# A two-layer recurrent and attention trunk on one core: split weights in their own tiles, other banks, norm sums on VectorE, masks at once, sixteen unread matmuls

## The chip, the core and the metric

The kernel runs on one core of a Trainium2 chip. The core has a matrix engine (TensorE, "PE"; its weight loads are listed as "PEld"), VectorE ("DVE"), ScalarE ("ACT"), GpSimd ("POOL") and SyncE ("SP"), whose queue issues nearly all transfers here. The metric is the device time of one launch in microseconds (us). The kernel before took 2058.51 us, the median of 3 runs from 2057.19 to 2059.92.

## The reference

Input and output are 512 tokens of 2048 features in float32. There are two residual layers.

- Layer A (HGRN2): RMS norm; one product with a 2048 x 8192 weight gives q, the forget logits, v and a gate; a gated linear recurrence in 16 heads of 128; a norm per head; times SiLU of the gate; a 2048 x 2048 output product; plus the residual.
- Layer B (forgetting attention): RMS norm of the new stream; keys, values and forget sums from one weight, queries and a gate from another; causal softmax attention in 16 heads with a decay term; a norm per head; times SiLU of the gate; a 2048 x 2048 output product; plus the residual.

```
proj = rmsnorm(x, norm_w) @ w_in
o = head_rmsnorm(recurrence_or_attention(...), out_norm_w)
x = x + (o * silu(gate)) @ w_out
```

All products are needed to float32 accuracy. The kernel splits each operand into a high part (rounded to the matrix engine's type) and a low part (the rest) and adds three products: high by high, high by low and low by high.

## The kernel before, in words

Activations are kept as 16 tiles of 128 features x 512 tokens. A *group* (function `group`, line 215) computes 512 output columns: 16 steps of 128 input features, each with 12 matmuls of 512 columns into four PSUM banks (three matmuls for each bank). At step 0 the group takes the banks gm0 to gm3; after step 15 `evac` empties each bank. There are 16 groups in stage "a" (the projections of layer A), 16 in stage "b", and an output product behind each.

*Weights.* `Chunks.load` (184) brings 512 KB, two steps' worth, into one of two raw buffers `wr` through SP's queue. `w_split` (139) makes the parts: ACT casts `wh`, DVE subtracts to get `wl` (`split`, 434: ACT in line 435, DVE in line 436; in stage b with scales, lines 147 and 148). Its tiles come from `w_tiles` (134): three of each in the pool of the current stage, two in the output products, where the same tag also serves the larger parts of the seven-product groups. `phase` (77) closes the pool of a stage and opens the next one on the same memory; a tile of the new pool waits for those tiles of the old one that lie where it lies.

*Output products* (`out_product`, 826). The first 512 outputs are a plain group; beside it `y_split` (780) splits the gated head outputs `Y`, and `quick_prep` (249) forms, for each pair of steps, sums of the quarters of two tiles in `tm` (one buffer), three subtractions on DVE and one on POOL, and splits them to `th` and `tl`. The other 1536 outputs are six *seven-product groups* (`quick_groups`, 311, and `quick`, 264), each with 8 steps of 21 matmuls of 256 columns; this is Strassen's scheme in Winograd's form on 2 x 2 blocks. `w_sums` (153) forms the sums of the weight quarters in `wm`, `w_split_quick` (160) splits them. `quick_sum` (295) puts the seven products together: one copy on ACT (299) and seven operations on DVE (300 to 309), with three temporaries `t`. Groups 0, 2 and 4 use the gm banks, groups 1, 3 and 5 the four `mx` banks (`bank`, 70). The last evacuation of layer A's product is held back and called in the third step of stage b's first group (`last_a`, line 849).

*Norms* (`Norm`, 337). `add` squares a tile on ACT (349) and adds it to a running sum on POOL (350); `finish` sums over partitions on PE. The first norm is added up in `load_x` (464) in the first group of stage a, beside the split of x (469, 470). The second is added up in `x1_done` (805), as each tile of the new stream X1 comes out of layer A's product. `x1_split` (847) splits X1 in the first group of stage b and calls `finish` in the last step.

*The start.* SP is asked for two tiles of x (256 KB each), the first weights (512 KB), two more tiles of x, and eight small vectors. Ten masks for the recurrence are made by POOL (a fill and two selections each, 514, 515 and 519) and cast by DVE (523), one mask for each step of the first group from the fourth on (`setup`, 472).

*Order.* Besides the groups, generators (`mix_a`, 599, and `mix_b`, 914) hold the work of the heads; `pump` advances them by so many pieces for each step. The program is laid down in this order, and a planner (`schedule_with_timeline_sim`, line 1087) then sets each engine's order for good: an instruction that is early in the program comes first, and a later one is moved into a gap where the plan has its operands and its tile ready. On the chip each engine follows its order and waits where the plan was too early. `hold` (226) keeps the last step of a stage from splitting the first weights of the next.

Of the kernel before, what the change touches and what calls it, by code (L numbers as in the profile page):

```python
# [10 lines left out]
F32R = mybir.dt.float32r  # L11
U8 = mybir.dt.uint8
# [4 lines left out]
P = 128  # L17
T = 512
D = 2048
KT = 16  # L20
H = 16
# [11 lines left out]
def hgrn2_fox(ctx, tc, io):  # L33
    nc = tc.nc
# [5 lines left out]
    cur = {}  # L40
# [4 lines left out]
    def nt(tag, shape, bufs, dt=F32, pool=None):  # L45
        uid[0] += 1
        return padded(pool or sb, shape, dt, tag, f"{tag}_{uid[0]}", bufs)
# [10 lines left out]
    def const(tag, shape, dt=F32):  # L58
        return padded(cp, shape, dt, tag, tag)
# [5 lines left out]
        return t.bitcast(F32)  # L65

    def tmp():
        return mt("t", (P, T), 4)

    def bank():  # L70
        return nt("mx", (P, T), 4, pool=ps)

    def mt(tag, shape, bufs=1, dt=F32):

        return nt(tag, shape, bufs, dt, cur["sb"])

    def phase(name):
        if cur:
            cur["ctx"].close()
        cur["ctx"] = c = ExitStack()  # L80
        cur["quick"] = name[0] == "o"
        cur["sb"] = c.enter_context(tc.tile_pool(name=f"sb{name}", bufs=1, reuse_waits="tile"))

    phase("a")
# [46 lines left out]
    load_vec("a_norm_w", S)  # L131


    def w_tiles(shape):

        n = 2 if cur["quick"] else 3
        return mt("wh", shape, n, F32R), mt("wl", shape, n, F32R)

    def w_split(r, kt, scales):
        h, l = w_tiles((P, T))  # L140
        if scales is None:
            split(r, h, l)
        else:
            n = T // len(scales)
            for i, w in enumerate(scales):
                c = slice(i * n, (i + 1) * n)
                S.activation(h[:, c], r[:, c], AF.Copy, scale=w[:, kt : kt + 1])  # L147
                V.scalar_tensor_tensor(  # L148
                    l[:, c], r[:, c], w[:, kt : kt + 1], rd(h)[:, c], op0=ALU.mult, op1=ALU.subtract
                )  # L150
        return h, l
# [8 lines left out]

    def w_split_quick(r, m):

        h, l = w_tiles((P, 2, 7, P))
        split(r[:, :, 1:4, :], h[:, :, 0:3, :], l[:, :, 0:3, :])
        split(m, h[:, :, 3:7, :], l[:, :, 3:7, :])
        return [(h[:, i, :, :], l[:, i, :, :]) for i in range(2)]

    class Chunks:
# [12 lines left out]
            for k in range(KT // 4):  # L181
                self.todo.append((ap[k], True, None, 0))

        def load(self):

            if not self.todo:
                return
            ap, quick, scales, kt = self.todo.pop(0)
            r = nt("wr", (P, 2 * T), 2)
            nc.sync.dma_start(r, ap)  # L190
            if quick:
                self.raw.append((lambda r=r.rearrange("p (a b c) -> p a b c", a=2, c=P): w_split_quick(r, w_sums(r)), 2))
            else:
                for i in range(2):
                    self.raw.append((lambda v=r[:, i * T : (i + 1) * T], k=kt + i: [w_split(v, k, scales)], 1))

        def split(self):
            if self.raw:
                fn, _ = self.raw.pop(0)
                self.parts.extend(fn())  # L200
# [48 lines left out]
    def quick_prep(p, y):  # L249

        k1, k2 = 2 * p, 2 * p + 1
        b11, b12, b21, b22 = y[k1][:, :TN], y[k1][:, TN:], y[k2][:, :TN], y[k2][:, TN:]
        m = mt("tm", (P, 4, TN), 1)
        V.tensor_sub(m[:, 0, :], b12, b11)
        G.tensor_sub(m[:, 2, :], b12, b22)
        V.tensor_sub(m[:, 1, :], b22, m[:, 0, :])
        V.tensor_sub(m[:, 3, :], b21, m[:, 1, :])
        th = mt(f"th{p}", (P, 3, TN), 1, F32R)
        tl = mt(f"tl{p}", (P, 3, TN), 1, F32R)
        split(m[:, 0, :], Xh[k1][:, TN:], Xl[k1][:, TN:])  # L260
        split(m[:, 1:4, :], th, tl)
        return th, tl
# [48 lines left out]
    def quick_groups(prep, residual, evac, hold):  # L311

        for u in range(6):
            k = 4 + 2 * u
            r = [residual(k), residual(k + 1)]
            banks = [nt(f"gm{j}", (P, T), 1, pool=ps) if u % 2 == 0 else bank() for j in range(4)]
            end = quick(banks, prep, lambda *p, k=k, r=r: evac(k, r, p), hold and u == 5)
            if u < 5:
                end()
        return end  # L320
# [16 lines left out]
    class Norm:  # L337
# [6 lines left out]
        def add(self, x):  # L344
            if self.n == 0:
                S.activation(self.acc, x, AF.Square)
            else:
                q = nt("z", (P, T), 4)
                S.activation(q, x, AF.Square)
                G.tensor_add(self.acc, self.acc, q)  # L350
            self.n += 1

        def finish(self):
# [98 lines left out]
    def fetch_x():  # L452
        kt = len(xs)
        if kt < KT:
            xs.append(nt(f"y{kt}", (P, T), 1))
            nc.sync.dma_start(xs[kt], io["x"][kt])

    for kt in range(2):
        fetch_x()
    wts.load()  # L460
    fetch_x()
    fetch_x()

    def load_x(kt):
        fetch_x()
# [37 lines left out]
    setup.append(lower_bounds)  # L503


    def mask(name, m, d, q0):
        n = 4 - q0
        g = P // (4 * m)
        u = const(name, (P, g * n * m), U8)

        def make():
            f = tmp()
            fv = f[:, : g * n * m].rearrange("p (g q r) -> p g q r", g=g, q=n)
            G.memset(f[:, : g * n * m], 1.0)
            G.affine_select(
                out=fv, in_=fv, pattern=[[-4 * m, g], [-m, n], [0, m]], compare_op=ALU.is_ge,
                fill=0.0, base=m * (d - q0), channel_multiplier=1,
            )
            G.affine_select(
                out=fv, in_=fv, pattern=[[4 * m, g], [m, n], [0, m]], compare_op=ALU.is_ge,  # L520
                fill=0.0, base=m * (q0 - d) + m - 1, channel_multiplier=-1,
            )
            V.tensor_copy(u, f[:, : g * n * m])

        setup.append(make)
        return u

    masks = {(1, 0): mask("m1_0", 1, 0, 0)}
    for m in (1, 4, 16):
        for d in (1, 2, 3):  # L530
            masks[m, d] = mask(f"m{m}_{d}", m, d, d)
    ats = [const(f"at{i}", (P, NW, P)) for i in range(2)]
    setup.append(lambda: [V.memset(t, 0.0) for t in ats])

# [269 lines left out]

    def x1_done(kt):
        nc.sync.dma_start(x1_d[kt], X1[kt])
        norm1.add(X1[kt])

    def out_a_evac():
        res = [res_a(j) for j in range(4)]  # L810
# [36 lines left out]
    def x1_split(kt):  # L847
        if kt == 2:
            last_a()
        if kt == 6:  # L850
            forget_weights()
        h, l = new_x(kt)
        split(X1[kt], h, l)
        X1[kt] = None
        if kt == KT - 1:
            norm1.finish()
# [2 lines left out]
    wfs = mt("wfs", (P, KT, 48), 1, F32R)  # L859

    def forget_weights():
        wf = mt("t", (P, KT, H), 4)
        nc.sync.dma_start(wf, io["wb_f"])
        V.memset(wfs.bitcast(F32), 0.0)
        V.tensor_mul(wf, wf, view(nk, 0, [[1, KT], [0, H]]))
        V.tensor_copy(wfs[:, :, 0:H], wf)
        V.tensor_sub(wfs[:, :, 32 : 32 + H], wf, rd(wfs)[:, :, 0:H])
# [224 lines left out]
```

## Time and profile before

The profiled execution took 2057.41 us, of which its span is 2055.4.

| quantity | value |
|---|---|
| PE busy | 1986.9 us, 97% |
| DVE busy | 1585.9 us, 77% |
| ACT busy | 1133.1 us, 55% |
| POOL busy | 305.6 us, 15% |
| mean granted clock of PE | 0.987 |
| bytes moved | 195 MB, 95 GB/s |
| PE idle for weight parts cast by ACT (`wh`) | 36.5 us in 3 waits |

How to read it. A row of the order of time is: start in us, duration in us, engine, line of the kernel, operation, output<-inputs, shapes and, behind "x", how many instructions are merged. In brackets stands the idle time of the engine ahead of it and what ended that. Matmuls overlap, so a matmul's duration (0.39 us) is longer than its distance to the next (0.23). The waits list the idle time of one engine by what ended it: total, times, longest. The stages list busy time of each engine between two times, with the granted clock of PE (1.00 is full, about half is the lowest seen) and what the transfers did. A row of one line gives the minimum, median and maximum duration in ns, the first and last start in us, and the shapes.

### The profile page before, as it was taken

Reading aid. Unit: us, or ns where it says so; the run is one execution under the profiler, and the core shown is the slowest. Engines: PE = TensorE matmul, PEld = TensorE weight load, DVE = VectorE, ACT = ScalarE, POOL = GpSimd, SP = SyncE. Lnnn points to the kernel's source line nnn. Section 1 sums busy time; section 2 is a strip of 40 time slices with the busy share of each in tenths; the row PEclk is TensorE's granted clock in tenths of the full one; section 3 lists DMA queues with packets and bytes.
Section 4 is the critical chain, followed back from the end, with each engine's and each line's share of the span. In section 5 each row is a group of like instructions: output and inputs, shape, how many; then the busy total and the mean of one; then the engine's idle time right before and its main releaser. Section 6 shows DMA issues by size and latency. Waiting matters only on the chain.

```text
span 2055.4 us, 28924 instructions
## 1 busy us (share of the span) xinstructions
PE 1986.9 (97%) x10202; PEld 1696.2 (83%) x10202; DVE 1585.9 (77%) x3250; ACT 1133.1 (55%) x2312; POOL 305.6 (15%) x404
## 2 busy tenths in 40 slices
PE   7999999999999999889999999999999999997998
PEld 5888888888888888779987888888888888885898
DVE  8778977989799889688984667666766666687787
ACT  5656655656566466644453555554555556564333
POOL 7303210313133031121110000010001000011000
PEclk9999999999999999989999999999999999998999
DMA  5222222222222222234433233223222322222453
GB/s 170 88 83 74 71 84 81 75 80 83 74 81 72 73 83 73 81 96 151 159 115 95 91 93 97 88 79 101 93 88 92 92 90 90 90 86 72 135 173 103
DMA packets 61408, 195.01 MB, mean 95 GB/s; under 512 B 7872, under 2 KB 8000, under 8 KB 61264
## 3 DMA queue, kind: packets, MB, share of 16 engines
q1 hardware_dynamic: 61120, 193.17, 30.0%
q8 instruction: 80, 1.31, 0.3%
q14 instruction: 64, 0.52, 0.1%
q10 hardware_dynamic: 144, 0.01, 0.0%
HBM read 184.73 MB, written 8.42 MB: 94 GB/s over the span
## 4 chain that ended last, share of the span: by engine, by line
PE 74%; DVE 13%; DMA 4%; issue 3%; ACT 3%; POOL 2%; SPq 0%; DVEq 0%; ACTq 0%; POOLq 0%
PE gm L237 16%; PE gm L239 16%; PE gm L238 16%; PE gm L234 5%; PE gm L233 5%; PE gm L235 5%; DVE wl L436 3%; DMA wr<-in_wa_q 2%; DMA wr<-in_wb_q 2%; PE mx L583 1%; PE mx L581 1%; PE mx L582 1%; DVE ml L436 1%; PE mx L430 1%; PE mx L431 1%
## 5 line engine op out<-in xcount | busy, mean ns | idle before, releaser
L237 PE MATMUL gm<-xh,wh 128*128 128x512 f32 x1664 | 654.2, 393 | 37.6 <-ACT wh L435 36.5
L238 PE MATMUL gm<-xl,wh 128*128 128x512 f32 x1664 | 653.5, 393 | 0.0
L239 PE MATMUL gm<-xh,wl 128*128 128x512 f32 x1664 | 605.8, 393 | 6.0 <-DVE wl L436 5.5
L237 PEld LDWEIGHTS gm<-xh,wh 128*128 128x128 f32 x1664 | 314.7, 189 | 102.9 <-ACT wh L435 37.6
L239 PEld LDWEIGHTS gm<-xh,wl 128*128 128x128 f32 x1664 | 312.4, 189 | 70.3 <-DVE wl L436 7.2
L238 PEld LDWEIGHTS gm<-xl,wh 128*128 128x128 f32 x1664 | 314.7, 189 | 63.5
L435 ACT CAST wh<-wr 128x512 fp32r<-128x512 f32 (+1 forms) x336 | 217.4, 650 | 217.6 <-PE gm L238 114.8
L436 DVE TENSOR_TENSOR wl<-wr,wh 128x512 fp32r<-128x512 f32 (+1 forms) x336 | 257.5, 770 | 75.5 <-ACT wh L435 60.7
L148 DVE SCALAR_TENSOR_TENSOR wl<-wr,v_b_norm_w,wh 128x256 fp32r<-128x256 f32 (+1 forms) x192 | 114.1, 596 | 137.5 <-ACT wh L147 129.2
L147 ACT ACTIVATE wh<-wr,v_b_norm_w 128x256 fp32r<-128x256 f32 (+1 forms) x192 | 111.8, 585 | 185.2 <-PE gm L238 144.0
L234 PE MATMUL gm<-wl,xh 128*128 128x512 f32 x512 | 201.5, 394 | 0.4 <-DVE wl L436 0.4
L235 PE MATMUL gm<-wh,xl 128*128 128x512 f32 x512 | 200.0, 392 | 0.0
L233 PE MATMUL gm<-wh,xh 128*128 128x512 f32 x512 | 183.6, 392 | 0.3 <-DVE q L547 0.2
L147 ACT ACTIVATE wh<-wr,v_kv_norm_w 128x256 fp32r<-128x256 f32 (+1 forms) x192 | 110.3, 574 | 59.4 <-PE gm L235 43.1
L148 DVE SCALAR_TENSOR_TENSOR wl<-wr,v_kv_norm_w,wh 128x256 fp32r<-128x256 f32 (+1 forms) x192 | 112.2, 586 | 35.8 <-ACT wh L147 35.3
L934 POOL TENSOR_SCALAR_AFFINE_SELECT s<-s 128x128 f32<-128x128 f32 x64 | 27.3, 427 | 647.7 <-DVE s L933 647.0
L576 DVE COPY_PREDICATED at<-m,mx 128x128 f32<-128x128 uint8 (+3 forms) x448 | 106.8, 297 | 11.2 <-PE mx L583 10.7
L233 PEld LDWEIGHTS gm<-wh,xh 128*128 128x128 f32 x512 | 96.0, 188 | 20.4 <-ACT wh L435 0.5
L234 PEld LDWEIGHTS gm<-wl,xh 128*128 128x128 f32 x512 | 96.3, 188 | 19.5 <-DVE wl L436 1.0
L235 PEld LDWEIGHTS gm<-wh,xl 128*128 128x128 f32 x512 | 96.3, 188 | 18.4
L435 ACT CAST kh<-k 128x512 fp32r<-128x512 f32 (+1 forms) x96 | 56.5, 588 | 52.3 <-PE mx L582 19.2
L385 POOL TENSOR_TENSOR z<-z,t 128x512 f32<-128x512 f32 x32 | 46.4, 1460 | 230.3 <-ACT t L384 230.3
(217 smaller groups left out, 3890.4 us busy)
## 6 DMA issues: line engine op xcount, KB each, us to landing
wr<-in_wa_qf SPq DMA_DIRECT2D x64, 512.0 KB, 3.5
wr<-in_wb_qk SPq DMA_DIRECT2D x64, 512.0 KB, 3.5
wr<-in_wa_v SPq DMA_DIRECT2D x32, 512.0 KB, 3.5
wr<-in_wa_g SPq DMA_DIRECT2D x32, 512.0 KB, 3.5
wr<-in_wb_v SPq DMA_DIRECT2D x32, 512.0 KB, 3.5
wr<-in_wb_g SPq DMA_DIRECT2D x32, 512.0 KB, 3.5
wr<-in_wa_q SPq DMA_DIRECT2D x24, 512.0 KB, 3.6
wr<-in_wb_q SPq DMA_DIRECT2D x24, 512.0 KB, 3.6
```

What stands on the lines that cost most here:

```text
L147: S.activation(h[:, c], r[:, c], AF.Copy, scale=w[:, kt : kt + 1])
L148: V.scalar_tensor_tensor(l[:, c], r[:, c], w[:, kt : kt + 1], rd(h)[:, c], op0=ALU.mult, op1=ALU.subtract)
L233: PE.matmul(banks[j], xh, h, start=f, stop=False)
L234: PE.matmul(banks[j], xh, l, start=False, stop=False)
L235: PE.matmul(banks[j], xl, h, start=False, stop=e)
L237: PE.matmul(banks[j], h[:, c], Xh[kt], start=f, stop=False)
L238: PE.matmul(banks[j], h[:, c], Xl[kt], start=False, stop=False)
L239: PE.matmul(banks[j], l[:, c], Xh[kt], start=False, stop=e)
L385: G.tensor_mul(z, z, l)
L435: S.copy(h, src)
L436: return V.tensor_sub(l, src, rd(h))
L576: V.copy_predicated(out, mv, data)
```

## The change

1. `w_tiles` goes. `w_split` takes `wh` and `wl`, three of each, from a pool that lives through the whole kernel; the seven-product parts get tiles of their own, `w7h` and `w7l`, two of each, in the stage's pool.
2. The sums of `quick_prep` share the tag `wm` and its two buffers; the temporaries `t` are three instead of four in the output products.
3. Seven-product groups 0, 2 and 4 use the mx banks, groups 1, 3 and 5 the gm banks.
4. The norm's additions are done by DVE. The second norm's squares and additions move from `x1_done` to `x1_split`.
5. The first two weight loads come ahead of the first group, each as two halves with a tile of x between them.
6. The masks are one tile, made ahead of the first group: one fill, twenty selections, one cast.
7. Sixteen matmuls of 128 x 128 ones into an mx bank that nobody reads come ahead of everything else on PE.

```
 def tmp():
-    return mt("t", (P, T), 4)
+    return mt("t", (P, T), cur["t"])
...
 def phase(name):
-    cur["quick"] = name[0] == "o"
+    cur["t"] = 3 if name[0] == "o" else 4
...
+idle = bank()
+for i in range(16):
+    PE.matmul(idle[:, :P], ones, ones, start=True, stop=True)
...
 def w_split(r, kt, scales):
-    h, l = w_tiles((P, T))
+    h, l = nt("wh", (P, T), 3, F32R), nt("wl", (P, T), 3, F32R)
...
 def w_split_quick(r, m):
-    h, l = w_tiles((P, 2, 7, P))
+    h, l = mt("w7h", (P, 2, 7, P), 2, F32R), mt("w7l", (P, 2, 7, P), 2, F32R)
...
-def load(self):
+def load(self, between=None):
...
-    nc.sync.dma_start(r, ap)
+    if between:
+        nc.sync.dma_start(r[:, :T], ap[:, :T])
+        between()
+        nc.sync.dma_start(r[:, T:], ap[:, T:])
+    else:
+        nc.sync.dma_start(r, ap)
...
 def quick_prep(p, y):
...
-m = mt("tm", (P, 4, TN), 1)
+m = mt("wm", (P, 4, TN), 2)
...
 def quick_groups(prep, residual, evac, hold):
...
-banks = [nt(f"gm{j}", (P, T), 1, pool=ps) if u % 2 == 0 else bank() for j in range(4)]
+banks = [nt(f"gm{j}", (P, T), 1, pool=ps) if u % 2 else bank() for j in range(4)]
...
 def add(self, x):
...
-G.tensor_add(self.acc, self.acc, q)
+V.tensor_add(self.acc, self.acc, q)
...
-for kt in range(2):
-    fetch_x()
-wts.load()
 fetch_x()
+wts.load(fetch_x)
 fetch_x()
+wts.load(fetch_x)
...
+def make_masks():
+    f = mt("e", (P, 4 * T))[:, : sum(sizes)]
+    G.memset(f, 1.0)
+    at = 0
+    for (m, d, q0), size in zip(levels, sizes):
+        fv = f[:, at : at + size].rearrange("p (g q r) -> p g q r", g=g, q=n)
+        G.affine_select(out=fv, in_=fv, ...)
+        G.affine_select(out=fv, in_=fv, ...)
+        masks[m, d] = all_masks[:, at : at + size]
+        at += size
+    V.tensor_copy(all_masks, f)
+
+make_masks()
...
 def x1_done(kt):
     nc.sync.dma_start(x1_d[kt], X1[kt])
-    norm1.add(X1[kt])
...
 def x1_split(kt):
...
 h, l = new_x(kt)
 split(X1[kt], h, l)
+norm1.add(X1[kt])
```

More of the change, by code (lines that the diff above doesn't have):

```diff
@@ L131, in hgrn2_fox @@
     load_vec("a_norm_w", S)
-    def w_tiles(shape):
-        n = 2 if cur["quick"] else 3
-        return mt("wh", shape, n, F32R), mt("wl", shape, n, F32R)
+    idle = bank()
+    for i in range(16):
+        PE.matmul(idle[:, :P], ones, ones, start=True, stop=True)
     def w_split(r, kt, scales):
-        h, l = w_tiles((P, T))
+        h, l = nt("wh", (P, T), 3, F32R), nt("wl", (P, T), 3, F32R)
         if scales is None:
@@ L503, in hgrn2_fox @@
     setup.append(lower_bounds)
[L506 to L514, printed above, removed]
+    masks = {}
+    levels = [(1, 0, 0), *((m, d, d) for m in (1, 4, 16) for d in (1, 2, 3))]
+    sizes = [P // 4 * (4 - q0) for _, _, q0 in levels]
+    all_masks = const("masks", (P, sum(sizes)), U8)
+    def make_masks():
[3 more added lines that the diff above has]
+        for (m, d, q0), size in zip(levels, sizes):
+            n = 4 - q0
+            g = P // (4 * m)
+            fv = f[:, at : at + size].rearrange("p (g q r) -> p g q r", g=g, q=n)
             G.affine_select(
@@ L522, in make @@
             )
[L523 to L531, printed above, removed]
+            masks[m, d] = all_masks[:, at : at + size]
+            at += size
+        V.tensor_copy(all_masks, f)
+    make_masks()
     ats = [const(f"at{i}", (P, NW, P)) for i in range(2)]
@@ L861, in forget_weights @@
     def forget_weights():
-        wf = mt("t", (P, KT, H), 4)
+        wf = mt("t", (P, KT, H), cur["t"])
         nc.sync.dma_start(wf, io["wb_f"])
```

## The prediction

> **What bounds the kernel now.** I read the page first, then the waits of TensorE, then the busy time by stage, and then the order of time around each hole.
>
> ```profile
> PE 1986.9 (97%) x10202; PEld 1696.2 (83%) x10202; DVE 1585.9 (77%) x3250; ACT 1133.1 (55%) x2312; POOL 305.6 (15%) x404
> PE   7999999999999999889999999999999999997998
> DVE  8778977989799889688984667666766666687787
> PEclk9999999999999999989999999999999999998999
> ```
>
> TensorE (PE) is busy for 1986.9 of 2055.4 us, so at most 68.5 us of idle time plus the time at a low clock can go. The second row says where it lies: in the first slice (51 us each), near slice 17 and near slice 36. The profiled execution took 2057.41 us (span 2055.4 and 2.0 around it), 1.1 below the median of 2058.51. The sum below is made against 2057.41 and 1.1 is added at its end.
>
> PE's waits, summed (us in total, times, longest):
>
> ```profile
> PE gm L237 <- ACT wh L435: 36.5, 3, 14.7
> PE gm L239 <- DVE wl L436: 5.5, 3, 4.1
> PE gm L290 <- DVE z L1003: 2.8, 1, 2.8
> PE gm L290 <- DVE y L814: 2.8, 1, 2.8
> ```
>
> Three waits for the first weight part make 36.5 us: the start and the entries to the two output products. Two waits of 2.8 us stand before the first seven-product group of each output product. The stages, with the columns of the first line:
>
> ```profile
> core 0: us, PE busy (x) PEld busy (x) DVE busy (x) ACT busy (x) POOL busy (x), PEclk, DMA share, GB/s
> 7.65:18.00 10.35, 10.35 (x39) 8.20 (x40) 9.92 (x20) 7.26 (x16) 9.13 (x13) 1.00 0.80 274
> 30.00:44.00 14.00, 9.86 (x35) 7.59 (x33) 13.97 (x10) 4.87 (x9) 12.05 (x8) 0.76 0.22 67
> 866.50:881.20 14.70, 0.04 (x1) 0.04 (x1) 11.55 (x13) 9.95 (x19) 7.13 (x5) 0.64 0.16 38
> 881.20:892.00 10.80, 10.80 (x41) 8.82 (x42) 9.29 (x17) 5.10 (x9) 0.92 (x1) 0.86 0.43 120
> 892.00:926.40 34.40, 34.40 (x152) 28.16 (x151) 26.69 (x46) 15.94 (x26) 5.30 (x6) 1.00 0.32 100
> 926.40:932.00 5.60, 2.81 (x14) 2.81 (x14) 5.60 (x9) 3.27 (x5) 1.51 (x2) 0.70 0.63 225
> 945.00:1045.00 100.00, 97.24 (x796) 95.62 (x795) 89.07 (x126) 44.05 (x55) 14.22 (x9) 1.00 0.45 142
> 1045.00:1066.00 21.00, 17.66 (x109) 16.21 (x109) 18.21 (x29) 11.54 (x21) 1.80 (x1) 0.84 0.31 103
> 1875.80:1882.00 6.20, 6.20 (x17) 4.88 (x18) 4.96 (x10) 2.70 (x5) 0.00 (x0) 0.58 0.51 158
> 1882.00:1921.00 39.00, 39.00 (x174) 32.30 (x173) 30.53 (x52) 17.83 (x28) 6.22 (x7) 1.00 0.30 92
> ```
>
> In 892 to 926 PE issues 152 matmuls of 512 columns in 34.40 us, 0.226 us each: a twelve-matmul step takes 2.72 us, a group of 192 takes 43.5 us. Everything is measured against that pace.
>
> **The change part by part.**
>
> *Weight parts in own tiles.* The first output product, in the order of time (start, duration; ACT, ACT, DVE, PE):
>
> ```profile
> 858.11 0.62 ACT L435 CAST wh<-wr 128x512 fp32r<-128x512 f32 x1 [1.53 <-PE gm L238]
> 865.18 1.31 ACT L367 ACTIVATE t<-z 128x512 f32<-128x512 f32 x2 [6.45 <-DVE z L381]
> 864.46 2.73 DVE L381 TENSOR_TENSOR z<-gm,rstd 128x512 f32<-128x512 f32 x4 [5.00 <-PE gm L239]
> 880.49 1.13 ACT L435 CAST wh<-wr 128x512 fp32r<-128x512 f32 x2
> 881.16 0.80 PE L237 MATMUL gm<-xh,wh 128*128 128x512 f32 x1 [14.71 <-ACT wh L435]
> 854.04 5.77 SPq L190 DMA_DIRECT2D wr<-in_wa_o  x2
> ```
>
> The raw weights were asked for by 859.8 and ACT stands idle for 6.45 us up to 865.18, yet the first cast for the new stage starts at 880.49, behind the last gate evacuation. The tile it writes belongs to the stage's own pool, which opens on memory that the gate evacuation's temporaries still hold. With wh and wl in the persistent pool its only conditions are the raw weights and the slot of three steps earlier, so it fits into those 6.45 us. The banks are no obstacle: the four L381 products that empty them start at 864.46 and each follows its own bank. So PE goes on at 866.5 and 14.7 us go. With them goes the low clock behind the hole: 10.80 us for 41 matmuls that need 9.3, 1.5 us. Sum 16.2.
>
> The second output product has the same picture:
>
> ```profile
> 1875.75 0.79 PE L237 MATMUL gm<-xh,wh 128*128 128x512 f32 x1 [14.11 <-ACT wh L435]
> ```
>
> It gives 14.1, and at a mean clock of 0.58 the next 6.20 us do 3.6 us of work: 2.6. Sum 16.7.
>
> What is late next is VectorE (DVE). The sums for the seven-product groups and the splits of this group are work that PE's advance doesn't remove. In the first product DVE had 9.29 + 26.69 = 36.0 us to do between 881.2 and 926.4. About 2.4 of it (four casts' remainders, some 0.6 each by the pitch of the DVE rows) fits into the 3.1 us that it idles in 866.5 to 881.2. The rest ends at 881.2 + 33.6 = 914.8, while PE would be through its group at 866.5 + 43.5 = 910.0: 4.8 us late. In the second product 4.96 + 30.53 = 35.5, less 2.4, from 1875.8 is 1908.9, against 1861.6 + 43.5 = 1905.1: 3.8 late. Two slots for the sums of quick_prep instead of one let DVE run at this pace. Together 8.6 us are given back. The bounds are zero (PE can begin the next group with the first of eight sums) and 16 (DVE falls as far behind again in the next group).
>
> Three temporaries instead of four cost nothing there: quick_sum takes three at a time and is called once in 20 us (168 matmuls of 256 columns at 97.24 / 796 = 0.12 us each).
>
> *Other banks for the first seven-product group.*
>
> ```profile
> 929.22 0.55 PE L290 MATMUL gm<-xh,wh 128*128 128x256 f32 x1 [2.79 <-DVE y L814]
> ```
>
> This group no longer waits for the evacuation of the plain group: 2.8 us, and 1.1 of low clock behind it (fourteen matmuls in 2.81 us, 0.20 each instead of 0.12). Twice, so 7.8 us.
>
> But the order is turned round for all six groups: the sixth now uses the gm banks, which the first group of the next stage takes at once, while the call that empties them stands in its third step.
>
> ```profile
> 1065.74 0.57 ACT L299 COPY t<-mx 128x512 f32<-128x512 f32 x1
> 1069.21 0.68 DVE L305 TENSOR_TENSOR t<-mx,t 128x512 f32<-128x512 f32 x1
> 1064.04 0.40 PE L237 MATMUL gm<-xh,wh 128*128 128x512 f32 x1
> ```
>
> Before, PE started the next group at 1064.04, 1.7 us ahead of the first read of the old banks. Now its first bank is free at 1066.3 and its last at 1069.9: 2.3 to 5.9 us of wait. Queued behind it on PE is the whole group. After the second product nothing follows, so it costs nothing there.
>
> *Norm sums on VectorE, later.* GpSimd (POOL) loses 30 additions.
>
> ```profile
> 27.73 14.87 POOL L350 TENSOR_TENSOR rstd<-rstd,z 128x512 f32<-128x512 f32 x9
> 29.48 5.23 DVE L470 SCALAR_TENSOR_TENSOR xl<-y,v_a_norm_w,xh 128x512 fp32r<-128x512 f32 x3
> 23.67 0.81 DVE L470 SCALAR_TENSOR_TENSOR xl<-y,v_a_norm_w,xh 128x512 fp32r<-128x512 f32 x1
> 36.44 2.07 PE L239 MATMUL gm<-xh,wl 128*128 128x512 f32 x4 [4.14 <-DVE wl L436]
> ```
>
> While POOL adds, a DVE instruction takes 1.74 us (5.23 over three) instead of 0.81. That makes DVE busy for 13.97 of 14 us in 30 to 44 and is what PE waits for: 5.5 us in the three waits, and 2.0 us of low clock (35 matmuls kept PE busy for 9.86 us instead of 7.9, at a mean clock of 0.76). On DVE one addition is about 0.6 us; 15 of them make 9 us in a group of 43.5, in which DVE's two splits a step cost 1.3 of 2.72. So 7.5 us go.
>
> In the second norm the squares and additions move from the seven-product groups to the first group of the next stage. They stand right behind the splits of X1, which the planner has put into the gaps of the sixth group, where DVE is busy for 18.21 of 21 us and PE already lost 3.3 us. Some of the 9 us will be in the way there; POOL's additions, which slowed DVE, no longer are. With the bank wait I take +3.0 for this boundary, near the bank wait's lower end, because the weight casts can now be done earlier; the bounds are -4 (all its present loss goes) and +12 (5.9, 2.5 of low clock, 3.5 of additions).
>
> *Weights and x in halves, sixteen matmuls, masks at once.*
>
> ```profile
> 6.98 1.14 ACT L435 CAST wh<-wr 128x512 fp32r<-128x512 f32 x2 [1.04 <-DMA wr<-in_wa_qf]
> 3.57 0.63 ACT L346 ACTIVATE rstd<-y 128x512 f32<-128x512 f32 x1 [1.49 <-DMA y<-in_x]
> 7.65 0.80 PE L237 MATMUL gm<-xh,wh 128*128 128x512 f32 x1 [7.65 <-ACT wh L435]
> ```
>
> The first weights landed at 6.98 behind two x tiles, 1 MB in all; the first x tile at 3.57. The second 256 KB now carry all that the first step needs, and should land near 4.7, by a third of the way: PE starts 2.3 us earlier. The next load is now one ahead in the order of SyncE's queue, but there are two raw buffers as before, so it can't start earlier.
>
> The sixteen matmuls run where PE is idle anyway. In 7.65 to 18 the 39 matmuls take 10.35 us instead of 8.8, the first of them 0.80 by its row where a later one takes 0.39: what a clock released in advance saves lies between 0 and 1.5, and I take 0.7. [...]
>
> ```profile
> L515 POOL TENSOR_SCALAR_AFFINE_SELECT t<-t x10: 313/672/1393, 2.2 to 24.6; 128x96 f32<-128x96 f32 x3, 128x64 f32<-128x64 f32 x3, 128x32 f32<-128x32 f32 x3, 128x128 f32<-128x128 f32 x1
> L519 POOL TENSOR_SCALAR_AFFINE_SELECT t<-t x10: 252/660/1822, 5.7 to 27.1; 128x96 f32<-128x96 f32 x3, 128x64 f32<-128x64 f32 x3, 128x32 f32<-128x32 f32 x3, 128x128 f32<-128x128 f32 x1
> L523 DVE CAST m<-t x10: 168/784/1298, 10.8 to 29.4; 128x96 uint8<-128x96 f32 x3, 128x64 uint8<-128x64 f32 x3, 128x32 uint8<-128x32 f32 x3, 128x128 uint8<-128x128 f32 x1
> ```
>
> Of the masks (minimum, median and maximum in ns) POOL does the same 20 selections, some 14 us, now in one piece from about 2, and DVE one cast instead of ten. That cast waits for all of them; behind it in DVE's queue stand splits that PE needs. If the planner puts it behind their true end, near 16, it costs about the 1.3 of the longest cast now; I take back 2.5 of this stage for it and for the added DVE work. Start: 7.5 + 2.3 + 0.7 - 2.5 = 8.0 us gained, bounds 0 and 11.5.
>
> Sum: -8.0 - 16.2 - 16.7 + 8.6 - 7.8 + 3.0 = -37.1. 2057.4 - 37.1 = 2020.3, and with the 1.1 a median of 2021.
>
> **The rivals.**
>
> *DVE becomes the bound of the output products.* For it: 89.07 of 100 us busy. Against it: what stretched it there were POOL's additions. Then the 16 of the bound are given back instead of 8.6, and the boundary costs 12: 2021 + 7 + 9 = 2037.
>
> *The cast of the masks stalls DVE at the start.* If it stands in DVE's queue ahead of the second step's split, PE ready at 5.3 does one step of 2.7 us and then waits from 8 to about 17: 9 us. The start's gain is gone, 2021 + 9 = 2030. For it: the cast is first in the program's order. Against it: the first of the ten casts stands at 10.8 today, with nothing in that line's view that it waited for.
>
> *The casts still wait.* If it was ACT's order that held the first weight part back, and not the memory, both entries stay as they are: 2021 + 32.9 - 8.6 = 2045. Against it speak the 6.45 us of idle ACT with the weights in place.
>
> *Slower: the low clock becomes the rule in the seven-product groups.* At 1045 to 1066 waits of a microsecond for wl made PE idle for 3.3 us and put the clock at 0.84, another 3.4: 6.7 us. If DVE, without slack, does this in every one of the twelve groups, eleven more cost 74 and the end is 2095; it decides from six groups on (6 x 6.7 is over 37.1). Against it: in 945 to 1045 the same DVE load leaves the clock at 1.00.
>
> **How the numbers follow.** Forecast 0.64, DVE as the bound 0.15, masks 0.11, casts still waiting 0.05, slower 0.05. Low end: start 11.5, nothing given back, boundary -4: 2021 - 3.5 - 8.6 - 7 = 2002. High end: the DVE case and a little, 2040. This leaves out the last two cases and some of the second. A measurement of this kernel can tell about 0.2%, 4 us. Where the casts still wait and the masks stall as well, the end is 2054 and can't be told from no change: 0.02 of that case. Faster 0.93, within 0.2% 0.02, slower 0.05.
>
> **What would show it.** Right: no wait for wh over 2 us near 866 and 1861; PE at work from about 5; no POOL additions in line 350, and DVE's splits at 0.8 up to 44 us; the first seven-product groups start without a wait for line 814 or 1003. PE's new waits are for wl and th at the start of these groups, and for line 299 to 305 at the next stage's first matmuls. Wrong: a cast of wh still behind line 384, PE idle over 8 us before 20, a clock under 0.9 through 945 to 1045, or DVE at 98% through both output products.

## The result, and the profile after

| | before | after |
|---|---|---|
| median of four runs each, side by side | 2057.85 us (2054.95 to 2059.92) | 2028.09 us (2025.90 to 2030.14) |
| ratio | | 0.9856, 95% interval 0.9839 to 0.9873 |
| profiled execution, its span | 2057.41, 2055.4 | 2028.22, 2026.5 |

The change is worth 29.8 us by the medians and 28.9 us by the two spans. The forecast was 37.1 less: 2021 in a range of 2002 to 2040. Direction and range hold, and 8.2 us by the spans are missing. The first rows of the page after:

```profile
PE 1985.9 (98%) x10218; PEld 1697.4 (84%) x10218; DVE 1567.6 (77%) x3271; ACT 1129.0 (56%) x2312; POOL 271.9 (13%) x365
PE   9999999999999999989989999999999999999898
PEclk9999999999999999999999999999999999999899
```

PE has sixteen matmuls more and one microsecond less of busy time, and its idle time has fallen from 68.5 to 40.6 us. The deep dips in the first slice and in slice 37 are gone; weak ones are left in slices 18, 21 and 38, and in the last one as before. PE's waits after (what waits, tile, line, what for; us in total, times, longest):

```profile
PE mx L295 <- ACT w7h L440: 8.4, 2, 4.3
PE gm L244 <- DVE wl L441: 3.9, 6, 1.7
PE gm L295 <- ACT w7h L440: 3.4, 1, 3.4
PE gm L297 <- DVE w7l L441: 3.0, 5, 1.2
PE mx L297 <- DVE w7l L441: 2.8, 3, 1.7
PE gm L242 <- ACT t L304: 1.7, 1, 1.7
PE gm L242 <- ACT wh L440: 0.3, 1, 0.3
```

The three waits for the first weight part, 36.5 us before, are 0.3. The two waits of 2.8 us for the evacuations before the seven-product groups are gone as well, but the row at the top has taken their place: twice, over 4 us each, the same matmul line waits for the split of the summed weights. The stages after (first line: the columns):

```profile
core 0: us, PE busy (x) PEld busy (x) DVE busy (x) ACT busy (x) POOL busy (x), PEclk, DMA share, GB/s
30.00:44.00 14.00, 13.82 (x61) 11.10 (x60) 10.52 (x17) 4.47 (x8) 0.00 (x0) 1.00 0.47 150
866.50:881.20 14.70, 13.04 (x58) 10.29 (x57) 14.70 (x23) 6.44 (x13) 5.89 (x5) 1.00 0.60 179
886.00:901.00 15.00, 15.00 (x68) 12.41 (x67) 14.65 (x28) 7.58 (x13) 6.68 (x4) 1.00 0.24 72
901.00:912.00 11.00, 5.17 (x27) 3.95 (x25) 10.04 (x18) 4.38 (x6) 0.00 (x0) 0.87 0.42 136
920.00:1020.00 100.00, 99.80 (x831) 99.60 (x831) 83.01 (x132) 39.99 (x48) 0.00 (x0) 1.00 0.46 144
1020.00:1035.00 15.00, 10.37 (x80) 9.55 (x78) 15.00 (x27) 11.88 (x21) 0.00 (x0) 1.00 0.27 98
1035.00:1045.00 10.00, 7.30 (x34) 6.80 (x35) 9.31 (x15) 6.33 (x13) 0.00 (x0) 0.66 0.34 118
```

In 30 to 44 PE now issues 61 matmuls where it issued 35. In the old hole, 866.5 to 881.2, it issues 58 where it issued one. The losses are in the rows below: 5.83 us of idle PE in 901 to 912, where the seven-product groups begin, and 7.3 in 1020 to 1045, at the crossing into the next stage. In both DVE is busy for over 90% of the time.

Where the 28.9 us come in is read from instructions that both kernels have, by how much earlier each starts:

| instruction | before | after | lead |
|---|---|---|---|
| first query evacuation | 60.61 | 51.60 | 9.0 |
| last gate evacuation of stage a | 864.46 | 855.82 | 8.6 |
| first seven-product group, its evacuating copy | 949.61 | 930.47 | 19.1 |
| fifth seven-product group, the same | 1033.79 | 1011.59 | 22.2 |
| first query evacuation of stage b | 1106.84 | 1088.83 | 18.0 |
| last gate evacuation of stage b | 1859.40 | 1841.74 | 17.7 |
| second product, first copy | 1944.95 | 1916.21 | 28.7 |
| end of the span | 2055.4 | 2026.5 | 28.9 |

So the start gives 9.0, the first product's entry with its first seven-product group 10.5, the groups after it 3.1, the crossing takes 4.2 back, and the second product gives 11.0. Small drifts make up the rest.

### The profile page after: what moved, and what is told of

It is laid out like the page before. It is cut to its first block, busy times and chain, and to the rows that moved or that the text cites. A ratio compares the mean times of both kernels' runs of the same rounds, so it can differ in the third digit from the quotient of the medians.

```text
span 2026.5 us, 28907 instructions
## 1 busy us (share of the span) xinstructions
PE 1985.9 (98%) x10218; PEld 1697.4 (84%) x10218; DVE 1567.6 (77%) x3271; ACT 1129.0 (56%) x2312; POOL 271.9 (13%) x365
## 4 chain that ended last, share of the span: by engine, by line
PE 71%; DVE 14%; DMA 6%; issue 3%; ACT 3%; POOL 3%; SPq 0%; DVEq 0%; ACTq 0%; POOLq 0%
PE gm L242 15%; PE gm L244 15%; PE gm L243 15%; PE gm L239 5%; PE gm L238 5%; PE gm L240 5%; DMA wr<-in_wb_q 3%; DVE wl L441 2%; DMA wr<-in_wa_q 2%; DVE w7l L441 2%; PE mx L587 1%; PE mx L585 1%; PE mx L586 1%; DVE ml L441 1%; PE mx L435 1%
## 5 line engine op out<-in xcount | busy, mean ns | idle before, releaser
L244 PE MATMUL gm<-xh,wl 128*128 128x512 f32 x1664 | 613.2, 392 | 4.4 <-DVE wl L441 3.9
L441 DVE TENSOR_TENSOR wl<-wr,wh 128x512 fp32r<-128x512 f32 x288 | 213.2, 744 | 67.7 <-ACT wh L440 57.8
L440 ACT CAST wh<-wr 128x512 fp32r<-128x512 f32 x288 | 177.2, 619 | 124.1 <-PE gm L243 89.8
L580 DVE COPY_PREDICATED at<-masks,mx 128x128 f32<-128x128 uint8 (+3 forms) x448 | 106.8, 297 | 11.2 <-PE mx L587 10.7
L440 ACT CAST w7h<-wr 128x768 fp32r<-128x768 f32 x48 | 40.1, 835 | 110.1 <-PE mx L296 45.3
```

The source lines that it names most:

```text
L244: PE.matmul(banks[j], l[:, c], Xh[kt], start=False, stop=e)
L440: S.copy(h, src)
L441: return V.tensor_sub(l, src, rd(h))
L580: V.copy_predicated(out, mv, data)
```

## The experiments

All ratios are to the kernel before, run beside each on the same chip, with a 95% interval. Differences in us between two variants are of their medians; the variants ran on three chips, on which the kernel before took 2057.0 to 2059.3 us, so such a difference across chips is good to about 2 us. Edits are to the kernel after unless said.

**Own tiles alone.** The kernel before, with only the weight parts in tiles of their own; to make room, three temporaries in the output products, and some small constants and the two score tiles of the recurrence in the first stage's pool.

```diff
-        h, l = w_tiles((P, T))
+        h, l = nt("wh", (P, T), 3, F32R), nt("wl", (P, T), 3, F32R)
...
-        h, l = w_tiles((P, 2, 7, P))
+        h, l = mt("w7h", (P, 2, 7, P), 2, F32R), mt("w7l", (P, 2, 7, P), 2, F32R)
```

> The kernel before with the weight parts in their own tiles alone (wh and wl in the lasting pool, w7h and w7l apart); the temporaries of the output products are three and some small constants of stage a move to its pool, for room. Old banks, old start, additions on GpSimd, quick_prep's sums in their own tm. The theory that the tiles are what held the entries back expects both waits of 14.7 and 14.1 us for wh to go and the start as before: 2058 - 33 plus up to 6 for VectorE, 2025 to 2031, with waits of up to 2.8 us for lines 814 and 1003 left. The rival, that the entries need the other parts of the change as well (the temporaries, the norm, the earlier loads), expects 2050 to 2058.

Measured: 2032.18 us (2030.76 to 2033.22), 0.9869 [0.9854, 0.9883], 27.2 below the 2059.34 of the runs beside it. The sum had 16.2 + 16.7 - 8.6 = 24.3 for this part, and the expectation 2025 to 2031, which it misses by 1.2. Three rows of its waits:

```profile
PE gm L237 <- ACT wh L435: 8.3, 1, 8.3
PE gm L290 <- DVE z L1003: 6.6, 1, 6.6
PE gm L290 <- DVE y L814: 5.2, 1, 5.2
```

Of the three waits for the first weight part only the one at the start is left. What held the casts back at the two entries was the memory of the tile they write. The waits before the seven-product groups have grown from 2.8 to 5.2 and 6.6: what PE gains at the entry, DVE gives back in part at the end of the group.

**The old bank order.** The seven-product groups take turns as before: the first waits for the plain group's banks, the sixth leaves them free for the next stage.

```diff
-            banks = [nt(f"gm{j}", (P, T), 1, pool=ps) if u % 2 else bank() for j in range(4)]
+            banks = [nt(f"gm{j}", (P, T), 1, pool=ps) if u % 2 == 0 else bank() for j in range(4)]
```

> The changed kernel with the old order of banks: gm for the seven-product groups 0, 2 and 4, mx for 1, 3 and 5. The prediction's sum has the new banks at -7.8 us for the two first groups and at 2.3 to 5.9 for stage b's first group, so it expects 2030 to 2034. The rival: PE waits for w7h there anyway, so the old wait for the evacuation hides under it, and only the wait at stage b's first group (1.7 and 0.9 us for lines 304 and 307, with some low clock) goes away: 2022 to 2027.

Measured: 2017.00 us (2015.94 to 2019.52), 0.9797 [0.9782, 0.9812]: 11.1 us faster than the kernel after. Undoing a part that should give 7.8 gains, by more than either side of the expectation allowed. Three rows of its waits:

```profile
PE gm L295 <- DVE z L1007: 5.8, 1, 5.8
PE gm L295 <- DVE y L817: 5.1, 1, 5.1
PE mx L297 <- DVE w7l L441: 1.2, 1, 1.2
```

The waits for the evacuation are back, and those for the first split of the summed weights are gone. The first copy stands at 928.85, 1.6 us earlier than after (in the runs below that change nothing at this place it scatters by about a microsecond, 930.29 to 931.48): the new order had only let PE start sooner and stop at the next thing that DVE delivers. The first query evacuation of the next stage starts at 1076.9 instead of 1088.8, so about 10 of the 11 us come from the crossing. PE there, in this kernel (start, duration):

```profile
1029.00 0.40 PE L242 MATMUL gm<-xh,wh 128*128 128x512 f32 x1
1030.62 0.39 PE L243 MATMUL gm<-xl,wh 128*128 128x512 f32 x1
1030.85 0.28 PE L297 MATMUL mx<-xh,w7l 128*128 128x256 f32 x1
```

```profile
1020.00:1035.00 15.00, 13.54 (x90) 12.23 (x89) 15.00 (x27) 10.25 (x19) 0.00 (x0) 1.00 0.26 81
1035.00:1045.00 10.00, 10.00 (x60) 8.81 (x59) 9.34 (x18) 7.55 (x17) 0.00 (x0) 1.00 0.34 118
```

Eight matmuls of the next stage (lines 242 and 243, gm banks) run from 1029.00 between those of the sixth group (mx banks), and 24 more, with line 244, before 1041. DVE is as busy as in the kernel after, but PE has something else to do while it waits. With the new order both want the gm banks. The first matmul of the next stage is then this one:

```profile
1035.21 0.39 PE L295 MATMUL gm<-th,w7h 128*128 128x256 f32 x1 [3.39 <-ACT w7h L440]
1044.76 0.50 PE L242 MATMUL gm<-xh,wh 128*128 128x512 f32 x1 [1.68 <-ACT t L304]
```

It waits only 1.68 us for its bank (second row, kernel after). The loss is not in that wait; it lies in the 3.39 us above it and the like, which nothing filled.

**New order, and the next stage's first group in the other banks.** If the conflict over the gm banks is the cause, this must bring the 10 us back with the new order in place.

```diff
-        banks = [nt(f"gm{j}", (P, T), 1, pool=ps) for j in range(4)]
+        banks = [bank() if own else nt(f"gm{j}", (P, T), 1, pool=ps) for j in range(4)]
...
-            norm1.finish()
+            norm1.finish(True)
-            group(qk_evac(2 * i), before=x1_split if first else None, rate=RATE_B)
+            group(qk_evac(2 * i), before=x1_split if first else None, rate=RATE_B, own=first)
```

(finish(True) puts the norm's two column sums in gm0 and gm1.)

> The changed kernel, new order of banks, but with stage b's first group in the mx banks and the two sums of its norm in gm banks, so that the last seven-product group and the group behind it don't share banks. Theory: what the new order costs is that TensorE can't put matmuls of stage b's group into the holes of the last seven-product group (with the old order 27 of them ran between 1029 and 1038). Then this kernel has the interleaving again and gains the 10 to 12 us that the old order gained: 2016 to 2019; the first seven-product group in mx instead of gm is worth nothing, since its weight parts are late. The prediction's view, that the new banks are worth 3.9 us at each first seven-product group, expects 2009 to 2013. A third, that the old order gained by something else, expects 2026 to 2030.

Measured: 2017.80 us (2017.57 to 2018.23), 0.9810 [0.9796, 0.9823]. The next stage's first query evacuation stands at 1079.7, 9.1 earlier than after, while the first copy, at 931.3, is no earlier. So the cost of the new order is the sharing of banks at the crossing, and it gives nothing at the start of the seven-product groups.

**Sums in a tile of their own.** In the kernel after, the sums of x (quick_prep) and of the weights (w_sums) share two slots of one name. The first run is the control: only the two tiles that make room.

```diff
-    ats = [const(f"at{i}", (P, NW, P)) for i in range(2)]
+    ats = [mt(f"at{i}", (P, NW, P)) for i in range(2)]
```

> The changed kernel with the two score tiles of the recurrence (ats, 4 KB for each partition) in the pool of stage a instead of the pool of constants. It only makes room for the next kernel, and nothing else differs. Every theory expects the changed kernel's time: 2028 within 4 us, and PE's waits for w7h ahead of the first seven-product groups at 4.0 and 4.3 us as before.

Measured: 2027.87 us (2026.67 to 2031.56), 0.9846 [0.9830, 0.9863]: no difference. With that, and

```diff
-        m = mt("wm", (P, 4, TN), 2)
+        m = mt("tm", (P, 4, TN), 1)
```

> The kernel of e1 with the sums of quick_prep in a tile of their own again (tm, one buffer, as before the change), so that they no longer share the two wm buffers with the sums of the weights. Theory A, the shared tag: the first sums of weights (line 156) wait for the slot of the last but one sums of quick_prep, started at 903.5 though their raw weights lay there from 898, and the wait of 4.0 to 4.3 us for w7h with the low clock behind it hangs on that. Then line 156 starts near 899, both waits fall under 1 us and the time falls by 10 to 14 us, to 2014 to 2018. Theory B, VectorE's throughput: it has the same work in the same time, some other piece of it is late, and the time stays at 2028 within 3 us. Theory C, the raw weights: the second load of seven-product weights lands at 905 in both, PE waits for its parts instead, and 3 us at most are gained: 2025.

Measured: 2023.40 us (2022.70 to 2024.44), 0.9827 [0.9812, 0.9841], 4.5 less than the control, and between what the expectation had for the shared slots (2014 to 2018) and for the raw weights (2025) or VectorE's pace (2028 within 3). The first weight sum, after and here:

```profile
902.55 0.94 DVE L441 TENSOR_TENSOR tl<-wm,th 128x768 fp32r<-128x768 f32 x1
903.53 0.69 DVE L156 TENSOR_TENSOR wm<-wr 128x512 f32<-128x512 f32 x1
```

```profile
896.46 0.68 DVE L156 TENSOR_TENSOR wm<-wr 128x512 f32<-128x512 f32 x1
912.32 0.58 PE L295 MATMUL mx<-th,w7h 128*128 128x256 f32 x1 [3.36 <-ACT w7h L440]
```

In the kernel after, the first weight sum starts as soon as the last but one sums of x have been read (902.55 and 0.94 make 903.49); here it starts 7 us earlier. But PE still waits 3.36 us, now for the second load's parts, with DVE busy for 10.97 of 11 us in 901 to 912. The shared slots are part of the cause; that the larger part is the amount of work on DVE is tried next.

**More work on DVE.** With the old bank order and the sums in a tile of their own (the edits as above, the two tiles that make room among them),

> The changed kernel with the old order of banks (2017.0 alone) and quick_prep's sums in a tile of their own (2023.4 alone, 4.6 us gained), with the score tiles in stage a's pool for room. If the two act on different waits (stage b's first group, and the first seven-product group of each output product) the gains add: 2012 to 2014. If both only shift the same backlog of VectorE ahead of the first seven-product group, or if the old wait for lines 817 and 1007 (5.1 and 5.8 us) hides what the own sums give, 2016 to 2018.

measured 2013.38 us (2013.16 to 2014.68), 0.9789 [0.9776, 0.9803]: 14.7 below the kernel after, where the two edits alone gave 11.1 and 4.5, so the gains add up within the 2 us. To this the last subtraction of quick_prep was added twice more:

```diff
         V.tensor_sub(m[:, 3, :], b21, m[:, 1, :])
+        V.tensor_sub(m[:, 3, :], b21, m[:, 1, :])
+        V.tensor_sub(m[:, 3, :], b21, m[:, 1, :])
```

> The kernel with old banks and own sums (2013.4), in which the last subtraction of quick_prep on VectorE is done three times instead of once: 16 more instructions of 0.33 us of pitch in each output product, 5.3 us, and nothing else; the result is the same. If VectorE's backlog is what holds the first seven-product groups, its added time goes to the end nearly whole: 8 to 11 us more, 2021 to 2024. If PE waits there for the order of some chain or for the raw weights and VectorE has slack, 0 to 3 us more: 2013 to 2016.

```profile
908.86 0.42 DVE L264 TENSOR_TENSOR tm<-y,tm 128x256 f32<-128x256 f32 x1
909.19 0.42 DVE L158 TENSOR_TENSOR wm<-wm,wr 128x256 f32<-128x256 f32 x1
```

These follow each other at 0.33 us, so 16 more per product are 5.3 us and 10.6 in all. Measured: 2024.64 us (2021.72 to 2025.79), 0.9832 [0.9818, 0.9845], 11.3 more by the medians and 9.0 by the spans (2011.5 and 2020.5). At the next stage's first query evacuation 3.0 of the 9.0 are there (1080.27 against 1077.28); the second product takes the other 6.0. Of the 5.3 us added to DVE in each product, then, a little over half comes out in the first and all of it in the second, some 85% of both together by the spans. The planner also laid PE's work down anew: the first copy stands 12.9 us later (941.96 against 929.04), the second only 1.5 (950.73 against 949.20), so the two products can't be read more finely than that. The expectation for slack on DVE, 0 to 3 us, is well exceeded: DVE's work is on the path at these two places, though the page has DVE at 77%.

**Both repairs with the new order.** The other way to combine them: the new order, the next stage's first group in the mx banks, and the sums in a tile of their own.

> Stage b's first group in the mx banks (2017.8 alone) with quick_prep's own sums (2023.4 alone, 4.5 us gained over the changed kernel). Both product orders of banks are free of sharing, and the first seven-product group needs no evacuation. If VectorE's backlog is the bound the new banks give nothing over the old ones: 2012 to 2015, as old banks with own sums (2013.4). If the waits of 4.9 and 7.4 us for lines 817 and 1007 in that kernel were a cost of their own, 2004 to 2010.

Measured: 2013.01 us (2011.78 to 2014.96), 0.9778 [0.9765, 0.9792]. This is the fastest kernel, though its interval overlaps that of the old order with own sums: even without the sharing, the new order for the first group is worth nothing that can be measured.

**Additions of the norm on POOL again,** in the places that they have after:

```diff
-                V.tensor_add(self.acc, self.acc, q)
+                G.tensor_add(self.acc, self.acc, q)
```

> The changed kernel with the norm's additions on GpSimd again, in their new places. The theory that GpSimd's additions stretch VectorE's instructions and so hold the first group expects VectorE instructions of 1.7 us between 20 and 45 again, waits for wl of 4 to 6 us in the first group, and 6 to 8 us more at the start; at stage b's first group, where VectorE is busy for all 15 us ahead of the boundary, either sign of 2 us. In all 2033 to 2038. The rival, that the start came from the earlier loads and the single mask cast, expects 2028 within 3.

Measured: 2043.96 us (2041.28 to 2046.22), 0.9933 [0.9919, 0.9946], 15.9 more, where the expectation had 2033 to 2038. First, DVE at the start, here and in the kernel after; then what POOL did here, over the whole kernel:

```profile
27.75 6.84 DVE L474 SCALAR_TENSOR_TENSOR xl<-y,v_a_norm_w,xh 128x512 fp32r<-128x512 f32 x4
```

```profile
28.97 1.41 DVE L474 SCALAR_TENSOR_TENSOR xl<-y,v_a_norm_w,xh 128x512 fp32r<-128x512 f32 x2
```

```profile
L355 POOL TENSOR_TENSOR rstd<-rstd,z 128x512 f32<-128x512 f32 x30 | 47.2, 1574 | 139.8 <-ACT z L354 138.2
```

The same split takes 1.71 us with POOL's additions beside it and 0.70 without. The first query evacuation starts at 60.19, 8.6 later, and the fifth seven-product copy at 1021.71, 10.1 later; the next stage's first query evacuation, at 1105.71, is 16.9 later, so 6.8 more are lost at the crossing, where the expectation had 2 of either sign. How POOL's additions stretch DVE's split, no run here shows.

**The sixteen matmuls, the loads, the masks.** Three parts of the start, each undone alone.

```diff
-    idle = bank()
-    for i in range(16):
-        PE.matmul(idle[:, :P], ones, ones, start=True, stop=True)
```

> The changed kernel without the sixteen unread matmuls. In the changed kernel the first twelve real matmuls still take 3.95 us (5.61 to 9.56) where a full clock needs 2.72, so the sixteen saved at most 0.2 of the 1.4 us that the start cost before. That theory expects no change: 2028 within 3 us, the first real matmuls between 5.3 and 5.8 and at full pace from about 8.3. The prediction's 0.7 us would give 2028.8, too near to be told apart by the time; the pace of the first matmuls tells it. The view that the sixteen release the clock in full expects 2.7 us of slow matmuls from the first one on instead of 2.3.

Measured: 2028.54 us (2027.64 to 2029.47), 0.9862 [0.9848, 0.9875]: no difference. PE at the start, after:

```profile
2.14 3.68 PE L136 MATMUL mx<-ones 128*128 128x128 f32 x16 [2.14 <-DVE ones L119]
5.61 2.02 PE L242 MATMUL gm<-xh,wh 128*128 128x512 f32 x4
8.66 1.07 PE L244 MATMUL gm<-xh,wl 128*128 128x512 f32 x4
```

and without the sixteen:

```profile
5.48 2.07 PE L239 MATMUL gm<-xh,wh 128*128 128x512 f32 x4 [5.48 <-ACT wh L437]
9.06 1.91 PE L241 MATMUL gm<-xh,wl 128*128 128x512 f32 x4
11.59 0.39 PE L239 MATMUL gm<-xh,wh 128*128 128x512 f32 x1
51.15 0.69 DVE L548 TENSOR_TENSOR q<-gm,rstd 128x512 f32<-128x512 f32 x1 [0.57 <-ACT rstd L337]
```

The sixteen bring the faster pace forward: four matmuls take 1.07 us from 8.66 on, and 1.91 without them at 9.06. (The expectation had full pace from about 8.3 without them too; it came at 11.4.) The time saved is not seen by the first evacuation, which stands at 51.15 without them and 51.60 with them. Between lies a stretch in which PE has slack, first in the kernel after, then without the sixteen:

```profile
18.00:30.00 12.00, 11.13 (x48) 8.44 (x47) 12.00 (x20) 12.00 (x23) 0.00 (x0) 1.00 0.56 204
```

```profile
18.00:30.00 12.00, 12.00 (x55) 9.94 (x53) 12.00 (x20) 12.00 (x23) 0.00 (x0) 1.00 0.68 251
```

DVE and ACT are busy throughout in both. After, PE (11.13 us, 48 matmuls) waits for them; without the sixteen it arrives with more left to do, does 55, and has caught up at the end.

```diff
+    for kt in range(2):
+        fetch_x()
+    wts.load()
     fetch_x()
-    wts.load(fetch_x)
     fetch_x()
-    wts.load(fetch_x)
```

> The changed kernel with the loads at the start in their old order and size (two x tiles, one whole weight load, two x tiles). The prediction gave the halves 2.3 us, so 2030.4. The theory that the first group is bound by VectorE, as the kernel without the sixteen matmuls showed (a clock released 3 us later, the first evacuation only 0.2 us later), expects part of it to vanish: first matmul near 7.6 instead of 5.6, first evacuation of a query 0 to 2 us later, 2028 to 2030.

Measured: 2028.79 us (2027.73 to 2030.96), 0.9855 [0.9842, 0.9870]. PE's first real matmul moves from 5.61 to 7.29 and the first evacuation from 51.60 to 52.64; of 1.7 us later, 1.0 is left there and nothing that the medians can tell.

Last, ten masks made one by one, each cast by itself as in the kernel before (with the control's two tiles moved):

```diff
...
-    make_masks()
...
+    masks = {(1, 0): mask("m1_0", 1, 0, 0)}
+    for m in (1, 4, 16):
+        for d in (1, 2, 3):
+            masks[m, d] = mask(f"m{m}_{d}", m, d, d)
```

> The changed kernel with the masks made one by one as before (ten casts, spread over the first group), and the score tiles in stage a's pool for room, which alone changed nothing (2027.9). In the changed kernel VectorE waited 0.6 us for the single cast. The prediction charged the single cast and the added additions 2.5 us together. If the single cast saves VectorE's nine other casts of up to 1.3 us, this kernel loses 0 to 3 us: 2028 to 2031. If waiting for twenty selections in one piece costs more than that, it gains up to 2.

Measured: 2029.88 us (2027.58 to 2030.20), 0.9857 [0.9844, 0.9870], first evacuation at 52.06. Against the control, 2.0 more by the medians with intervals that overlap: not told apart.

## Why the prediction was right, and where it was off

**Own tiles: right.** The tile's memory held the casts back, not ACT's order. Own tiles alone took both waits of 14 us away and gave 27.2 where 24.3 stood in the sum. The rest of the change was not needed for it. The rival in which the casts still wait fell with that row.

**The start: right in size.** 8.0 forecast, 9.0 at the first evacuation. But it is POOL's additions that make it: with them back, 8.6 of it is lost. Of the earlier loads and the sixteen matmuls, 2.3 + 0.7 of the sum, 1.0 and nothing are left at the first evacuation (52.64 and 51.15 without them, 51.60 with both); the rest ends in the slack behind ACT and DVE. The 2.5 taken back for the masks and DVE's additions was hardly owed: the mask cast waited 0.59 us for POOL. That the too large gains and the too large charge cancel is luck.

```profile
17.81 0.53 DVE L533 CAST masks<-e 128x704 uint8<-128x704 f32 x1 [0.59 <-POOL e L527]
```

The rival that had it stall DVE for 9 us fell.

**Other banks: the step that failed.** "This group no longer waits for the evacuation of the plain group: 2.8 us, and 1.1 of low clock behind it (fourteen matmuls in 2.81 us, 0.20 each instead of 0.12). Twice, so 7.8 us." The wait did go, and PE did start: the first such matmul, 929.22 before, stands at 903.51. What the step left out is what comes next in the same group:

```profile
903.51 0.28 PE L295 MATMUL mx<-xh,w7h 128*128 128x256 f32 x1
908.78 0.39 PE L295 MATMUL mx<-th,w7h 128*128 128x256 f32 x1 [4.04 <-ACT w7h L440]
912.17 0.58 PE L297 MATMUL mx<-th,w7l 128*128 128x256 f32 x1 [1.66 <-DVE w7l L441]
```

The evacuation and the weight sums are both DVE's work, and DVE was late with both, so taking one wait away uncovered the other. With the old order the first group ends 1.6 us sooner in the first product, hardly more than that row scatters: the term is at best nothing and at worst +1.6 there instead of -3.9, and about nothing in the second (the lead of the old order grows by 0.3). A part of the 4.04 us is not DVE's pace: in 901 to 912 DVE stood idle for 0.93 us, in its order, until ACT had cast the second load, which ACT itself had waited for.

**VectorE's give-back: right in size; what stood beside it was not.** Entry, banks and give-back together were to give 15.3 in the first product and 16.8 in the second; the copies show 10.5 and 11.0, 10.6 short in all. The entries less the give-back, 11.4 and 12.9, were right: with the old bank order and own sums the lead grows from the last gate evacuation (856.16 and 1830.18) to the first copy (929.04 and 1903.70) by 12.3 and 12.0, and with own tiles alone by 11.4 and 12.0 (865.31 to 939.08, 1848.38 to 1921.96). That is 24.3 and 23.4 where 24.3 was forecast. So 7.8 of the shortfall is the bank term, which the sum let stand beside the give-back as if the two did not overlap, and the rest fits the pair of slots that two kinds of sums share (4.5 by the time of the whole kernel): "Two slots for the sums of quick_prep instead of one let DVE run at this pace" saw the second slot and not that the weights' sums would use it too. That DVE's work is what is late there, the added subtractions show.

**The crossing: near by chance.** +3.0 forecast, 4.2 measured. The conflict over the gm banks was named, but priced as a wait of 2.3 to 5.9 us at the next stage's first matmul. That wait is 1.68 us. The price is 10 us, because those matmuls would otherwise have run inside the sixth group's holes, and the norm's additions leaving POOL (6.8 us there, by the run with them back) hid most of it. Before the change no matmul of the next stage ran before 1064.04, so the trace before did not show the filling, though it had the old order. The weight parts' own tiles are enough to let it begin: in the run with them alone, with the old order and POOL's additions where they were, the first matmul of the next stage stands 9.4 us ahead of the sixth group's copy, and 29 run before it:

```profile
1049.07 0.40 PE L237 MATMUL gm<-xh,wh 128*128 128x512 f32 x1
1058.51 0.58 ACT L299 COPY t<-mx 128x512 f32<-128x512 f32 x1
```

With the old order in the kernel after it stands 13.2 ahead (1029.00, copy at 1042.21). From the fifth copy to the next stage's first query evacuation the lead over the kernel before grows by 0.6 with own tiles alone (10.0 to 10.6) and by 6.0 there (23.9 to 29.9). What POOL's leaving and the other parts each add to that was not tried by itself.

**What the sum did not have:** 3.1 us between the first and the fifth seven-product group. 99.80 of 100 us are busy there with POOL idle, where 97.24 were with POOL's additions. The stretch took 84.2 us before and 81.1 after; with own tiles alone, POOL adding beside these groups as before, it took 84.7, and with the additions on POOL again but in their later place 81.6. In the other variants, in none of which POOL adds there, it is 79.9 to 82.2, leaving aside the run with the added subtractions. So the 3.1 go with the additions' leaving these groups.

**The slower case** did not come: the clock is 1.00 in 920 to 1020. Of the case in which DVE becomes the bound, a part came true, at the first seven-product groups and not throughout. Added up from the forecast's -37.1: the start -1.0, entry and banks +10.6, the inner groups -3.1, the crossing +1.2, drifts +0.5, which is -28.9.

## What to carry to other kernels

A wait that is taken away is worth only the distance to the next thing that is late on the same engine (here 2.8 us of wait went and 4.04 came); where both are delivered by one busy engine, count that engine's work and not the waits (5.3 us more of it in each product cost 9.0 by the spans). Two stages that meet should not want the same banks: what is lost is not the wait at the bank (1.68 us here) but the work that could have filled the other stage's holes (about 10). And a slot under a shared name joins two streams of work that had nothing to do with each other (4.5 us here).

## What was not expected of the hardware

Sixteen matmuls of 128 columns, each with a weight load of its own, took 3.68 us at the start, 0.23 each, as much as one of 512 columns later (0.226), and the granted clock reads 1.00 while matmuls of 512 columns run at 0.43. The pace changed about 6 us after PE's first matmul in the kernel after (2.14 to 8.3), in three other kernels with the sixteen and without the sixteen (5.48 to 11.4). In six more kernels with the sixteen it changed only near 10, with the old loads near 12, and in the kernel before 2.7 us after the first matmul (7.65 to 10.4). So with the new loads the sixteen bring the faster pace forward by 1 to 3 us. From the first matmul to the faster pace it thus took 2.7 us in the kernel before, about 6 in six kernels (with own tiles alone from 8.25 to 14.4) and 8 to 10 in seven; what sets this time was not shown.

POOL was slower too. Its subtraction for the sums took 0.92 us in the kernel before (first row) and 2.21 in the kernel after (second row, 4.42 for two), where DVE was busy for 14.65 of 15 us; over all sixteen of them the median is 0.91 before and 1.29 after:

```profile
887.50 0.92 POOL L255 TENSOR_TENSOR tm<-y,y 128x256 f32<-128x256 f32 x1 [8.77 <-DVE xl L436]
```

```profile
896.32 4.42 POOL L260 TENSOR_TENSOR wm<-y,y 128x256 f32<-128x256 f32 x2 [4.45 <-DVE tl L441]
```

That DVE's work is what holds it up, and which of its instructions, was not tried.
